# A decoder block with all large products by tokens, and every turn of a result through 32x32 DVE transposes and DRAM

## The chip, the cores and the metric

The kernel runs on one NeuronCore of a Trainium2 chip. The metric is the device time of one execution in microseconds (us). Engines are named as the profile names them: PE (TensorE, the matmuls), PEld (its weight loads), DVE (VectorE), ACT (ScalarE), POOL (GpSimd) and SP (SyncE, which issues transfers here).

## What is computed

One layer on 256 tokens of width 2048, all in float32: a half-step SwiGLU FFN (width 5632), a mixing block, a cross-attention into 256 memory tokens, a second half-step FFN, and a last RMSNorm. Cut to what matters:

```
h = h + 0.5 * swiglu(rms_norm(h, ffn1_norm), w_gate, w_up, w_down)        # (silu(x@w_gate) * (x@w_up)) @ w_down
n = rms_norm(h, mix_norm)
rq, rk, rv, rg, sq, sk, sv = split(n @ w_in)          # 8 heads of retention, 16 + 2 of sliding-window attention
ret = silu(rg) * group_norm(retention(rope(rq), rope(rk), rv))
swa = sliding_window_attention(rope(sq), rope(sk), sv, sinks)
h = h + concat(ret, swa) @ w_out
h = h + memory_cross_attention(rms_norm(h, xa_norm), rms_norm(mem, mem_norm), xa_wq, xa_wkv, xa_wo)   # 4 heads of 512
h = h + 0.5 * swiglu(rms_norm(h, ffn2_norm), ffn2_w_gate, ffn2_w_up, ffn2_w_down)
out = rms_norm(h, final_norm)
```

## The kernel before

**Precision.** Each float32 operand is cut into a high part, rounded to the matmul's format, and a low part, the rest (`halves`: ACT copies the high part, DVE subtracts). A product is three matmuls: high by high, high by low, low by high.

**The stream.** All weights pass once, in pieces of 128x1024 (0.5 MB). SP loads them two at a time into `wf` (three buffers, lines 149 to 161), ACT and DVE cut them into `wh` and `wl` (four buffers, `split`, line 163), and PE uses one piece per *step*. `run_stream` (188) goes through the steps of all *units* in one list; a unit is a set of output columns, summed over its blocks of 512 inputs in a PSUM tile `acc` (two of them). At each step it first runs what is due, then emits the split of the piece three steps ahead (`LOOKAHEAD`), then the step's matmuls. After a unit's last step `done` is called. `later(n, f)` puts f n steps further in the program. Within the first 16 steps two units alternate, and everything is pinned in order there; beyond that a scheduler sets each engine's order.

**Two kinds of step.** *By tokens* (`by_tokens`, 224): the activation's 128 tokens are PE's stationary operand, 512 weight columns move past, and the result has tokens on the partitions: 2 x 2 x 3 = 12 matmuls of 512 columns (lines 408 to 410). *By weights* (`by_weights`, 235): a 128x128 weight tile is stationary, and the activation's high and low parts of 256 tokens move past together: 8 matmuls of 512 columns (243), then 8 of 256 for the low weights (251). The result has features on the partitions, as the next product wants its inputs; the two column halves are summed afterwards (`total`, 399; `add_to_h`, 413). By weights go both down projections of FFN 1, retention's rq and rk, `w_out`, and the keys, queries and output of the cross-attention. The residual `h` lies with features on the partitions (`hT`).

**The turn that exists already.** FFN's gated block comes by tokens and is wanted by features. `up_done` (448) lets DVE transpose its 32x32 squares into `box`, 16 moves on SP's queue (`move`, 459, two to five steps later) shift the squares between partitions, and `made` (464, seven steps later) splits the result. After the cross-attention, `turn_h` (886) turns `h` back with 32 PE transposes.

**Norms.** A norm's scale is applied late. `stat` squares each block on ACT and sums on DVE; after the last one `finish` (line 371) sums over the partitions with four matmuls on PE and takes the power on Pool. `attend` (821) is one head of the cross-attention; `ret_scores` (686) the retention scores of one head.

Of the kernel before, what the change touches and what calls it, by code (L numbers as in the profile page):

```python
# [17 lines left out]
P = 128  # L18
# [13 lines left out]
WARM = 12  # L32
FIRST = 16
SWA_EVERY = 5
# [3 lines left out]
def decoder_block(ctx: ExitStack, tc: tile.TileContext, a: dict, out: bass.AP):  # L38
# [5 lines left out]
    small = ctx.enter_context(tc.tile_pool(name="small", bufs=8))  # L44
    ps_acc = ctx.enter_context(tc.tile_pool(name="ps_acc", bufs=2, space=bass.MemoryType.PSUM))
# [36 lines left out]

    nc.scalar.dma_start(gains, a["gains"])
# [8 lines left out]

# [36 lines left out]
    class Unit:  # L129
# [4 lines left out]
        def __init__(self, w, index, n, lhs, done, blocks, turned=False, per_half=False, pair=False):  # L134
            self.w, self.n, self.lhs, self.done = w[2 * index : 2 * index + 2] if pair else w[index], n, lhs, done
            self.blocks, self.turned, self.per_half, self.pair = list(blocks), turned, per_half, pair
            units.append(self)
# [10 lines left out]

    def load(w, piece, count):
        wf = wpool.tile([P, 2, 1024], F32, tag="wf", name=nm("wf"), bufs=3)  # L150
        nc.sync.dma_start(wf[:, :count, :], w[piece : piece + count].rearrange("c p n -> p c n"))
        return [wf[:, i, :] for i in range(count)]

    def load_pair(w, piece, cuts=(0, 1024)):

        wf = wpool.tile([P, 2, 1024], F32, tag="wf", name=nm("wf"), bufs=3)
        src = w[:, piece].rearrange("f p n -> p f n")
        for lo, hi in zip(cuts, cuts[1:]):
            nc.sync.dma_start(wf[:, :, lo:hi], src[:, :, lo:hi])
        v = wf.rearrange("p f (k n) -> p k f n", n=S)  # L160
        return [v[:, 2 * i : 2 * i + 2] for i in range(2)]

    def split(wf, n, parts):
        wh, wl = (wpool.tile([P, 1024], F32R, tag=x, name=nm(x)) for x in ("wh", "wl"))
        if len(wf.shape) == 4:
            dst = [x.rearrange("p (k f n) -> p k f n", k=2, f=2) for x in (wh, wl)]
            for i in range(parts):
                ks = slice(i * 2 // parts, (i + 1) * 2 // parts)
                halves(dst[0][:, ks], dst[1][:, ks], wf[:, ks])
        else:  # L170
# [5 lines left out]
    def pin():  # L176

        prev = {}
        for ins in nc.cur_bb.bb.instructions:
            if ins.engine in prev:  # L180
# [7 lines left out]
    def run_stream():  # L188
        steps = [x for u in units for x in u.steps()]
        steps[:FIRST] = [x for y in zip(steps[: FIRST // 2], steps[FIRST // 2 : FIRST]) for x in y]  # L190
        loaded = []
        for i in range(0, FIRST, 4):
            cuts = (0, 512, 1024) if i == 0 else (0, 1024)
            for lo, hi in zip(cuts, cuts[1:]):
                load_x(i // 4, lo // S, hi // S)
                if i == 0:
                    if lo == 0:
                        wf = wpool.tile([P, 2, 1024], F32, tag="wf", name=nm("wf"), bufs=3)
                        src = steps[0][0].w[:, steps[0][3]].rearrange("f p n -> p f n")
                    nc.sync.dma_start(wf[:, :, lo:hi], src[:, :, lo:hi])  # L200
            if i == 0:
                v = wf.rearrange("p f (k n) -> p k f n", n=S)
                both = [[v[:, 2 * j : 2 * j + 2] for j in range(2)]]
            else:
                both = [load_pair(steps[i][0].w, steps[i][3])]
            both.append(load_pair(steps[i + 1][0].w, steps[i + 1][3]))
# [4 lines left out]
        def prepare(upto):  # L211
            while nxt[0] < min(upto, len(steps)):
# [8 lines left out]
                ready[at] = split(loaded[at], steps[at][0].n, 2 if at == 0 else 1)  # L221
# [10 lines left out]

        wide_first = [True]

        def by_weights(acc, x, wh, wl, first, last):

            wide = first or (wide_first[0] and not last)
            wide_first[0] = not wide

            def main_pass(closing):  # L240
                for k in range(4):
                    for f in range(2):
                        nc.tensor.matmul(  # L243
                            acc[:, f, :], wh[:, k, f * P : (f + 1) * P], x[:, k, :, :],
                            start=first and k == 0, stop=closing and k == 3,
                        )

            def low_pass():
                for k in range(4):
                    for f in range(2):  # L250
                        nc.tensor.matmul(  # L251
                            acc[:, f, :S], wl[:, k, f * P : (f + 1) * P], x[:, k, 0, :], start=False, stop=False
                        )
            if wide:
                main_pass(False)
                low_pass()
            else:
                low_pass()
                main_pass(last)

        held = []
        for at, (u, b, ks, _, first, last) in enumerate(steps):
# [16 lines left out]
            if u.turned:  # L279
                by_weights(u.acc[0], x, wh, wl, first, last)  # L280
# [16 lines left out]
        run_until(lambda: not tasks)  # L297

# [30 lines left out]
    class Norm:  # L329
# [12 lines left out]
        def block(self, b, src):  # L342

            x = blk()
            k = 0
# [3 lines left out]
            self.blocks[b] = x  # L349
# [44 lines left out]
        def scale_turned(self, x):  # L394
# [4 lines left out]
    def total(acc):  # L399

        x = t2k().rearrange("p (f s) -> p f s", f=2)
        copy(x, acc[:, :, S:])
        nc.vector.tensor_tensor(x, acc[:, :, :S], x, ALU.add)  # L403
# [9 lines left out]
    def add_to_h(j, acc, factor):  # L413

        v = hT[j // 2][:, 2 * (j % 2) : 2 * (j % 2) + 2, :]
        x = t2k().rearrange("p (f s) -> p f s", f=2)
        copy(x, acc[:, :, S:], scale=factor)
        nc.vector.tensor_tensor(v, v, x, ALU.add)  # L418
        nc.vector.scalar_tensor_tensor(v, acc[:, :, :S], factor, v, ALU.mult, ALU.add)  # L419

    def to_h(w, lhs, factor, blocks, norm=None, then=None):

        def done(acc, j):
            add_to_h(j, acc, factor)
            if norm is not None and j % 2 == 1:
                norm.block(j // 2, [hT[j // 2]])
                norm.stat([hT[j // 2]])
            if then is not None:
                then(j)
        for j in range(8):  # L430
            Unit(w, j, 256, lhs, lambda acc, j=j: done(acc, j), blocks, turned=True)

    def ffn(norm, w_gate, w_up, down):
# [12 lines left out]
        def up_done(b):  # L446
            def done(acc):
                s = gated.pop(b)
                box = blk(F32).rearrange("p k c s -> p (k c s)").rearrange("p (w b n) -> p w b n", w=2, b=4)
                squares = box[:, 0].rearrange("p b (q t j) -> p q b t j", q=4, t=2)  # L450
                for t in range(2):
                    nc.vector.scalar_tensor_tensor(s[t], acc[:, t, :], norm.scale(t), s[t], ALU.mult, ALU.mult)  # L452
                    nc.vector.transpose(squares[:, :, :, t, :], s[t].rearrange("p (q b j) -> p q b j", q=4, b=4))  # L453
                for i in range(4):
                    later(2 + i, lambda i=i: move(box, i))
                later(7, lambda: made(b, box))
            return done

        def move(box, i):

            for j in range(4):
                nc.sync.dma_start(box[32 * j : 32 * j + 32, 1, i, :], box[32 * i : 32 * i + 32, 0, j, :])  # L462

        def made(b, box):
            x = blk()
            for t in range(2):
                src = box[:, 1].rearrange("p a (q t j) -> p q t a j", q=4, t=2)[:, :, t]
                hi, lo = (
                    x[:, :, c, t * P : (t + 1) * P].rearrange("p q (a j) -> p q a j", a=4) for c in range(2)
                )  # L470
                halves(hi, lo, src)
            acts[b] = x

        for g, fbs in enumerate((range(0, 6), range(6, 11))):
            for b in fbs:
                Unit(w_gate, b, 512, norm.blocks, gate_done(b), range(4), pair=True)
                Unit(w_up, b, 512, norm.blocks, up_done(b), range(4), pair=True)
            down(g, acts, fbs)
# [557 lines left out]
```

## Time and profile before

| | |
|---|---|
| median of 3 runs (lowest, highest) | 2222.48 us (2220.45, 2222.61) |
| the profiled execution, its span | 2222.29 us, 2220.5 us |
| mean granted TensorE clock | 0.997 |
| matmuls on lines 408, 409, 410 | 2112 each |
| matmuls on lines 243 and 251 | 1984 each |
| moved by DMA, mean rate | 427.04 MB, 192 GB/s |

A row of a group gives line, engine, operation, operands, shape and count, then busy us and mean ns of one, then the idle time of the engine just before, and what ended it. A row of a timeline gives start, length, what, and in brackets the idle time before it. ACTq, SPq and POOLq are the sequencers that issue transfers. In rows of DMA issues the last number is the median time in us from issue to landing.

### The profile page before, as it was taken

What the parts mean: (1) busy time and instruction counts of PE and PEld (TensorE: products, weight loads), DVE (VectorE), ACT (ScalarE), POOL (GpSimd) and SP (SyncE); (2) the same over time, 40 slices, a digit from 0 to 9 for tenths busy, and PEclk for the clock granted to TensorE, in tenths of its full rate; (3) what the DMA queues carried; (4) which work ended last, traced back from release to release, by engine and by line L of the source; (5) the groups of instructions that cost most, each with busy time, mean ns of one, the idle gap of its engine ahead of it and who ended that gap; (6) DMA issues with size and microseconds to landing.
All of it is one profiled execution on the core that took longest, in us unless ns stands there. A gap on an engine that the chain in (4) does not pass through costs nothing.

```text
span 2220.5 us, 27264 instructions
## 1 busy us (share of the span) xinstructions
PE 2199.1 (99%) x10898; PEld 1865.5 (84%) x10898; DVE 1290.8 (58%) x1540; ACT 1035.7 (47%) x1281; POOL 10.3 (0%) x17
## 2 busy tenths in 40 slices
PE   8999999999999999999999999999999999999998
PEld 7788888888888888888888889888888888888886
DVE  5555555455456678886765656664555554555554
ACT  5444434444445565555544554454444433444443
POOL 0000000000000000000000000000000000000000
PEclk9999999999999999999999999999999999999999
DMA  6556555565565554445555544454665565466563
GB/s 241 199 196 224 205 190 181 191 213 185 202 222 197 182 178 163 153 170 190 209 185 191 193 171 152 154 190 163 226 206 186 214 211 195 161 234 208 200 230 133
DMA packets 126527, 427.04 MB, mean 192 GB/s; under 512 B 12608, under 2 KB 23872, under 8 KB 126272
## 3 DMA queue, kind: packets, MB, share of 16 engines
q1 hardware_dynamic: 126256, 425.26, 55.2%
q8 instruction: 85, 1.39, 0.2%
q14 instruction: 42, 0.34, 0.0%
q10 hardware_dynamic: 144, 0.05, 0.0%
HBM read 411.62 MB, written 2.10 MB: 186 GB/s over the span
## 4 chain that ended last, share of the span: by engine, by line
PE 96%; SPq 1%; DMA 1%; DVE 1%; issue 1%; ACT 0%; ACTq 0%; POOLq 0%; POOL 0%
PE acc L410 21%; PE acc L409 21%; PE acc L408 21%; PE acc L243 20%; PE acc L251 10%; SPq L462 1%; DMA wf<-in_ffn_w_up 1%; PE tmp L408 0%; PE tmp L410 0%; PE tmp L409 0%; PE tmp L568 0%; DVE wl L73 0%; PE tmp L594 0%; ACT wh L68 0%; PE tmp L371 0%
## 5 line engine op out<-in xcount | busy, mean ns | idle before, releaser
L73 DVE TENSOR_TENSOR wl<-wf,wh 128x1024 fp32r<-128x1024 f32 (+1 forms) x773 | 936.8, 1221 | 721.0 <-ACT wh L68 715.0
L68 ACT ACTIVATE wh<-wf 128x1024 fp32r<-128x1024 f32 (+1 forms) x773 | 813.2, 1059 | 913.0 <-PE acc L410 609.7
L408 PE MATMUL acc<-wh,blk 128*128 128x512 f32 (+1 forms) x2112 | 821.0, 389 | 4.8 <-ACT wh L68 3.1
L409 PE MATMUL acc<-wl,blk 128*128 128x512 f32 (+1 forms) x2112 | 819.6, 388 | 2.2 <-DVE wl L73 2.2
L410 PE MATMUL acc<-wh,blk 128*128 128x512 f32 (+1 forms) x2112 | 819.4, 388 | 0.1
L243 PE MATMUL acc<-blk,wh 128*128 128x512 f32 x1984 | 480.8, 392 | 0.6 <-ACT wh L68 0.6
L408 PEld LDWEIGHTS acc<-wh,blk 128*128 128x128 f32 x2112 | 396.9, 188 | 86.1 <-ACT wh L68 3.9
L409 PEld LDWEIGHTS acc<-wl,blk 128*128 128x128 f32 x2112 | 397.1, 188 | 84.0 <-DVE wl L73 3.2
L410 PEld LDWEIGHTS acc<-wh,blk 128*128 128x128 f32 x2112 | 397.0, 188 | 81.9 <-DVE blk L327 0.5
L243 PEld LDWEIGHTS acc<-blk,wh 128*128 128x128 f32 x1984 | 364.3, 189 | 70.6 <-ACT wh L68 1.0
L251 PEld LDWEIGHTS acc<-blk,wl 128*128 128x128 f32 x1984 | 257.5, 192 | 15.1 <-ACT blk L68 4.9
L251 PE MATMUL acc<-blk,wl 128*128 128x256 f32 x1984 | 263.5, 284 | 3.8 <-ACT blk L68 3.8
L68 ACT ACTIVATE t2k<-acc 128x512 f32<-128x512 f32 x56 | 33.5, 598 | 126.0 <-PE acc L243 126.0
L418 DVE TENSOR_TENSOR h<-h,t2k 128x512 f32<-128x512 f32 x32 | 22.2, 693 | 53.7 <-ACT t2k L68 53.7
L73 DVE TENSOR_TENSOR blk<-blk,blk 128x512 fp32r<-128x512 f32 x44 | 28.5, 689 | 39.7 <-ACT blk L68 39.7
L68 ACT ACTIVATE blk<-blk 128x512 fp32r<-128x512 f32 x44 | 25.4, 625 | 52.2 <-DMA blk<-blk 52.2
L68 ACT ACTIVATE blk<-tmp 128x512 fp32r<-128x512 f32 (+3 forms) x57 | 26.0, 470 | 26.9 <-DVE blk L73 15.9
L452 DVE SCALAR_TENSOR_TENSOR t2k<-acc,n,t2k 128x512 f32<-128x512 f32 x44 | 31.1, 746 | 8.5 <-PE acc L410 8.5
L403 DVE TENSOR_TENSOR t2k<-acc,t2k 128x512 f32<-128x512 f32 x24 | 16.6, 690 | 32.9 <-ACT t2k L68 32.9
L443 ACT ACTIVATE t2k<-acc,n 128x512 f32<-128x512 f32 x44 | 27.6, 680 | 3.6 <-PE acc L410 3.3
L68 ACT ACTIVATE blk<-h,gains 128x256 fp32r<-128x256 f32 x64 | 28.2, 499 | 1.6 <-DVE h L419 1.6
L453 DVE STREAM_TRANSPOSE blk<-t2k 128x512 f32<-128x512 f32 x44 | 28.6, 686 | 0.0
(130 smaller groups left out, 612.1 us busy)
## 6 DMA issues: line engine op xcount, KB each, us to landing
wf<-in_ffn_w_up SPq DMA_DIRECT2D x88, 1024.0 KB, 5.4
wf<-in_ffn_w_gate SPq DMA_DIRECT2D x87, 1024.0 KB, 5.2
wf<-in_ffn_w_down SPq DMA_DIRECT2D x84, 1024.0 KB, 4.9
wf<-in_w_in_rqk SPq DMA_DIRECT2D x16, 1024.0 KB, 4.9
wf<-in_w_in_rvg SPq DMA_DIRECT2D x16, 1024.0 KB, 4.9
wf<-in_w_out SPq DMA_DIRECT2D x16, 1024.0 KB, 4.9
wf<-in_xa_wk SPq DMA_DIRECT2D x16, 1024.0 KB, 4.9
wf<-in_xa_wv SPq DMA_DIRECT2D x16, 1024.0 KB, 4.9
```

The source lines that it names most:

```text
L68: return nc.scalar.activation(dst, src, AF.Copy, **kw)
L73: nc.vector.tensor_tensor(lo, src, hi, ALU.subtract)
L243: nc.tensor.matmul(acc[:, f, :], wh[:, k, f * P : (f + 1) * P], x[:, k, :, :], start=first and k == 0, stop=closing and k == 3,)
L251: nc.tensor.matmul(acc[:, f, :S], wl[:, k, f * P : (f + 1) * P], x[:, k, 0, :], start=False, stop=False)
L408: nc.tensor.matmul(o, ah, bh, start=start, stop=False)
L409: nc.tensor.matmul(o, ah, bl, start=False, stop=False)
L410: nc.tensor.matmul(o, al, bh, start=False, stop=stop)
L418: nc.vector.tensor_tensor(v, v, x, ALU.add)
L443: nc.scalar.activation(gated[b][t], acc[:, t, :], AF.Silu, scale=norm.scale(t))
L452: nc.vector.scalar_tensor_tensor(s[t], acc[:, t, :], norm.scale(t), s[t], ALU.mult, ALU.mult)
L453: nc.vector.transpose(squares[:, :, :, t, :], s[t].rearrange("p (q b j) -> p q b j", q=4, b=4))
L462: nc.sync.dma_start(box[32 * j : 32 * j + 32, 1, i, :], box[32 * i : 32 * i + 32, 0, j, :])
```

## The change

Everything that went by weights goes by tokens, so it comes out with tokens on the partitions; a new `cross` turns it. For each half of 128 tokens DVE transposes the 32x32 squares of a 128x512 tile, Pool's queue writes the tile to DRAM (256 KB), and four reads from there (64 KB each, runs of 512 bytes) bring it back with rows of squares exchanged. What uses the result stands `TURN` = 4 steps later. `cross` serves the gated blocks (in place of `move`), `to_h`, rq and rk, keys, queries, and `turn_h`. `together` interleaves two units that follow on a turned result: all blocks of both but the last, then the last block of each. The first weight piece and the first `x` are loaded in smaller parts, the first 128 KB of `x` from ACT's queue, and SP's instructions are pinned to program order at the end.

```
-        def __init__(self, w, index, n, lhs, done, blocks, turned=False, per_half=False, pair=False):
+        def __init__(self, w, index, n, lhs, done, blocks, per_half=False, pair=False):
...
+                nx, ny = (sum(z[1] == s[-1][1] for z in s) for s in (x, y))
+                out += x[:-nx] + y[:-ny] + x[-nx:] + y[-ny:]
...
+                for j, lo, hi in ((0, 0, S), (0, S, 2 * S), (1, 0, 2 * S), (0, 2 * S, 1024), (1, 2 * S, 1024)):
+                    if j == 0 and lo > 0:
+                        load_x(0, lo // S, hi // S)
+                    nc.sync.dma_start(dst[j][:, :, lo:hi], src[j][:, :, lo:hi])
...
-            if u.turned:
-                by_weights(u.acc[0], x, wh, wl, first, last)
...
+        pin([mybir.EngineType.SP])
...
+    def cross(src, then, delay=TURN):
+        out = []
+        for v in src:
+            sq, dst = t2k(), t2k()
+            nc.vector.transpose(sq.rearrange("p (g q j) -> p q g j", g=4, q=4), v)
+            box = dram.tile([P, 512], F32, tag="box", name=nm("box"))
+            nc.gpsimd.dma_start(box, sq)
+            far = box.rearrange("(i r) (g n) -> g r i n", i=4, g=4)
+            for g in range(4):
+                nc.gpsimd.dma_start(dst[32 * g : 32 * g + 32, :].rearrange("p (i n) -> p i n", i=4), far[g])
+            out.append(dst.rearrange("p (i q j) -> p q i j", i=4, q=4))
+        later(delay, lambda: then(out))
+
+    def halves_of(out, x):
+        for t in range(2):
+            hi, lo = (x[:, :, c, t * P : (t + 1) * P].rearrange("p q (a j) -> p q a j", a=4) for c in range(2))
+            halves(hi, lo, out[t])
         return x
...
+            cross([squares_of(x) for x in s], add)
+        for b in range(4):
+            Unit(w, b, 512, lhs, lambda acc, b=b: done(acc, b), blocks, pair=True)
...
-                for i in range(4):
-                    later(2 + i, lambda i=i: move(box, i))
-                later(7, lambda: made(b, box))
+                def made(out):
+                    acts[b] = halves_of(out, blk())
+                cross([squares_of(x) for x in s], made)
...
+            s = [scaled(acc, t, 512, norm) for t in range(2)]
+            def made(out):
+                dst[i] = halves_of(out, blk())
                 if then is not None:
                     later(1, then)
-            later(1, finish)
+            cross([squares_of(x) for x in s], made)
...
-        tp = [tmp_ps() for _ in range(2)]
-        for t in range(2):
-            for k in range(4):
-                nc.tensor.transpose(tp[t][:, k * P : (k + 1) * P], hT[b][:, k, t * P : (t + 1) * P], ident)
-            copy(h[t][:, b * 512 : (b + 1) * 512], tp[t])
+        def made(out):
+            for t in range(2):
+                copy(squares_of(h[t][:, b * 512 : (b + 1) * 512]), out[t])
+        cross([hT[b][:, :, t * P : (t + 1) * P].rearrange("p q (a j) -> p q a j", a=4) for t in range(2)], made)
```

How the change moves instructions, at three places. First SP at the first down projection of FFN 1, before; `wf` are the loads of weights, `blk` the turn of the last gated block.

```order
L159 DMA wf_1917<-in_ffn_w_up 128x2x1024
L151 DMA wf_1951<-in_ffn_w_down 128x2x1024
L151 DMA wf_1985<-in_ffn_w_down 128x2x1024
L151 DMA wf_2029<-in_ffn_w_down 128x2x1024
L151 DMA wf_2079<-in_ffn_w_down 128x2x1024
L462 DMA blk_2003<-blk_2003 32x256 x16
L151 DMA wf_2129<-in_ffn_w_down 128x2x1024
L151 DMA wf_2181<-in_ffn_w_down 128x2x1024
```

SP there after the change:

```order
L178 DMA wf_1914<-in_ffn_w_up 128x2x1024
L178 DMA wf_1948<-in_ffn_w_down 128x2x1024
L178 DMA wf_1982<-in_ffn_w_down 128x2x1024
L178 DMA wf_2037<-in_ffn_w_down 128x2x1024
L178 DMA wf_2071<-in_ffn_w_down 128x2x1024
L178 DMA wf_2110<-in_ffn_w_down 128x2x1024
L178 DMA wf_2144<-in_ffn_w_down 128x2x1024
```

The 16 moves are gone from SP; the turn of a gated block now stands on Pool's queue as one write and four reads per half, in series.

Second, DVE between the end of a query's unit and its scores in the first `attend`, before: `acc` is the unit's sum, `wl` are splits of weights, line 403 is `total`, and line 833 is the maximum over the scores.

```order
L403 TENSOR_TENSOR t2k_10464<-acc_10379,t2k_10464 128x512
L397 TENSOR_TENSOR t2k_10464<-t2k_10464,rows_9058 128x512
L73 TENSOR_TENSOR wl_10468<-wf_10442,wh_10467 128x1024
L73 TENSOR_TENSOR wl_10494<-wf_10491,wh_10493 128x1024
L73 TENSOR_TENSOR blk_10397<-t2k_10464,blk_10397 128x2x256
L73 TENSOR_TENSOR wl_10549<-wf_10491,wh_10548 128x1024
L833 TENSOR_REDUCE xm_10538<-tmp_10513 128x2
```

DVE there after the change; line 417 is the transpose of one half in `cross`.

```order
L417 STREAM_TRANSPOSE t2k_9937<-t2k_9933 128x4x4x32
L75 TENSOR_TENSOR wl_9956<-wf_9915,wh_9955 128x1024
L75 TENSOR_TENSOR wl_9975<-wf_9972,wh_9974 128x1024
L417 STREAM_TRANSPOSE t2k_9946<-t2k_9935 128x4x4x32
L75 TENSOR_TENSOR wl_9991<-wf_9972,wh_9990 128x1024
L75 TENSOR_TENSOR wl_10009<-wf_10006,wh_10008 128x1024
L75 TENSOR_TENSOR blk_10024<-t2k_9938,blk_10024 128x4x128
L75 TENSOR_TENSOR wl_10030<-wf_10006,wh_10029 128x1024
L75 TENSOR_TENSOR wl_10083<-wf_10080,wh_10082 128x1024
L75 TENSOR_TENSOR blk_10024<-t2k_9947,blk_10024 128x4x128
L843 TENSOR_REDUCE xm_10070<-tmp_10045 128x2
```

Two transposes, two splits of weights apart, are new. Six splits of weights lie between the first of them and the maximum's row, where three lay between the sum and that row; the low part of each half stands four splits behind its transpose.

Third, PE at the same `attend`, before: `acc` rows are the next unit's steps, `tmp` rows of lines 408 to 410 are the scores.

```order
L243 MATMUL acc_10379<-blk_10278,wh_10375 128x512 x8
L243 MATMUL acc_10471<-blk_10144,wh_10402 128x512 x8
L251 MATMUL acc_10471<-blk_10144,wl_10403 128x256 x8
L251 MATMUL acc_10471<-blk_10187,wl_10423 128x256 x8
L243 MATMUL acc_10471<-blk_10187,wh_10422 128x512 x8
L408 MATMUL tmp_10513<-blk_9061,blk_10397 128x256
L409 MATMUL tmp_10513<-blk_9061,blk_10397 128x256
```

PE there after the change, from the last matmuls ahead of the scores:

```order
L434 MATMUL acc_9959<-wh_9974,blk_9739 128x512
L435 MATMUL acc_9959<-wl_9975,blk_9739 128x512
L436 MATMUL acc_9959<-wh_9974,blk_9739 128x512
L434 MATMUL tmp_10045<-blk_8764,blk_10024 128x256
L435 MATMUL tmp_10045<-blk_8764,blk_10024 128x256
L436 MATMUL tmp_10045<-blk_8764,blk_10024 128x256
```

Two steps of the next unit stood ahead of the scores; now it is five steps of 12 matmuls, 60 in all, and four more between the scores of the two halves of the tokens.

238 lines of the change are left out of this document (109 added, 129 removed).

## The prediction

> **What bounds the kernel now.** I read the page first: which engine fills the span, and what the chain that ended last is made of.
>
> ```profile
> span 2220.5 us, 27264 instructions
> PE 2199.1 (99%) x10898; PEld 1865.5 (84%) x10898; DVE 1290.8 (58%) x1540; ACT 1035.7 (47%) x1281; POOL 10.3 (0%) x17
> PE 96%; SPq 1%; DMA 1%; DVE 1%; issue 1%; ACT 0%; ACTq 0%; POOLq 0%; POOL 0%
> ```
>
> TensorE is busy 99% of the span and is 96% of the chain. So only two things can move the time: how long PE needs for the same products, and how long it stands still. Everything on DVE (58%), ACT (47%), the queues and Pool counts only where PE waits for it. The profiled execution took 2222.3 us, 1.8 more than its span; the median of the three runs is 2222.48, so the sum is made against 2222.3. About 0.2% (4.4 us) is what a measurement here can tell from no change.
>
> The second view is the groups: products by weights run from two lines.
>
> ```profile
> L243 PE MATMUL acc<-blk,wh 128*128 128x512 f32 x1984 | 480.8, 392 | 0.6 <-ACT wh L68 0.6
> L251 PE MATMUL acc<-blk,wl 128*128 128x256 f32 x1984 | 263.5, 284 | 3.8 <-ACT blk L68 3.8
> ```
>
> Matmuls overlap in the records, so 392 and 284 ns aren't prices. The price is the distance between starts. The chain, in order of time, gives it for the stage by weights (start, length, what):
>
> ```profile
> 301.41 1.91 PE acc L251 x16
> 303.32 3.65 PE acc L243 x16
> 306.98 1.91 PE acc L251 x16
> ```
>
> 16 narrow and 16 wide matmuls, two steps of the program, take 306.98 - 301.41 = 5.57 us: 2.78 us a step. The timeline of PE in a stage by tokens:
>
> ```profile
> 1599.81 0.39 PE L410 MATMUL acc<-wh,blk 128*128 128x512 f32 x1
> 1600.03 0.39 PE L408 MATMUL acc<-wh,blk 128*128 128x512 f32 x1
> ...
> 1616.81 0.39 PE L410 MATMUL acc<-wh,blk 128*128 128x512 f32 x1
> ```
>
> 75 starts lie between the first and the last of these rows: 17.00 / 75 = 0.2267 us. A step by tokens has 12 of them: 2.72 us.
>
> **The change part by part.**
>
> *All large products by tokens.* L243 has 1984 matmuls, 8 a step: 248 steps. Each becomes 12 matmuls of 512 columns in place of 8 of 512 and 8 of 256. The columns streamed are the same (6144); four matmuls fewer start. 248 x (2.783 - 2.720) = **-15.5 us**, all on the path, since PE is the path. [...]
>
> *The first units of both down projections of FFN 1.* Here PE stands still today, because the last gated block isn't turned yet:
>
> ```profile
> 291.51 1.11 PE L251 MATMUL acc<-blk,wl 128*128 128x256 f32 x8
> 295.16 2.07 PE L251 MATMUL acc<-blk,wl 128*128 128x256 f32 x8 [2.53 <-ACT blk L68]
> 651.37 0.73 PE L243 MATMUL acc<-blk,wh 128*128 128x512 f32 x2 [0.57 <-ACT wh L68]
> 653.36 2.08 PE L251 MATMUL acc<-blk,wl 128*128 128x256 f32 x8 [1.26 <-ACT blk L68]
> 281.98 10.31 SPq L462 DMA_DIRECT2D blk<-blk  x15
> 293.95 1.15 ACT L68 ACTIVATE blk<-blk 128x512 fp32r<-128x512 f32 x2 [2.99 <-DMA blk<-blk]
> ```
>
> Idle 2.53 and 0.57 + 1.26, 4.4 us. A unit has one step per block now and two after, so the last block is wanted after 10 and 8 steps instead of 5 and 4, 27 and 22 us. The round trip below needs about 16. **-4.4 us.** What is late next is nothing on PE: the weights no longer queue behind 16 moves on SP.
>
> *The moves leave SP.* Once they cost PE time away from a down projection, and the same rows measure how late ACT may be:
>
> ```profile
> 64.82 10.12 SPq L462 DMA_DIRECT2D blk<-blk  x16
> 71.04 1.06 ACT L68 ACTIVATE wh<-wf 128x1024 fp32r<-128x1024 f32 x1 [1.66 <-PE acc L410]
> 76.55 1.16 ACT L68 ACTIVATE blk<-blk 128x512 fp32r<-128x512 f32 x2 [4.45 <-DMA blk<-blk]
> 80.36 2.01 ACT L68 ACTIVATE wh<-wf 128x1024 fp32r<-128x1024 f32 x2 [2.66 <-DMA wf<-in_ffn_w_up]
> 82.74 0.50 PE L409 MATMUL acc<-wl,blk 128*128 128x512 f32 x1 [0.63 <-DVE wl L73]
> ```
>
> The split due at 71.04 + 2.72 = 73.76 came at 80.36, 6.6 us late, and PE lost 0.6: a split may be 6 us late for nothing. That is the cover of every ACT or DVE instruction that will wait for a round trip. **-0.6 us.** An issue on SP is 10.12/16 = 0.63 us.
>
> *turn_h.* Its 32 PE transposes go to DVE, eight at a time between two products:
>
> ```profile
> 1530.18 1.03 PE L892 MATMUL tmp<-ident,h 128*128 128x128 f32 x8
> 1530.97 0.48 PE L408 MATMUL acc<-wh,blk 128*128 128x512 f32 x1
> ```
>
> 4 x 0.79 = **-3.2 us**.
>
> *Smaller first loads.* PE's and ACT's first rows:
>
> ```profile
> 5.99 1.15 ACT L68 ACTIVATE wh<-wf 128x512 fp32r<-128x512 f32 x2 [3.54 <-DMA wf<-in_ffn_w_gate]
> 7.60 0.50 PE L408 MATMUL acc<-wh,blk 128*128 128x512 f32 x1 [1.73 <-ACT blk L68]
> 12.02 1.06 ACT L68 ACTIVATE wh<-wf 128x1024 fp32r<-128x1024 f32 x1 [3.27 <-DMA wf<-in_ffn_w_up]
> 13.13 0.50 PE L408 MATMUL acc<-wh,blk 128*128 128x512 f32 x1 [2.18 <-ACT wh L68]
> 14.39 0.50 PE L409 MATMUL acc<-wl,blk 128*128 128x512 f32 x1 [0.76 <-DVE wl L73]
> 18.38 0.40 PE L410 MATMUL acc<-wh,blk 128*128 128x512 f32 x1
> ```
>
> and the windows of 10 us (start:end, length, PE busy):
>
> ```profile
> 30.00:40.00 10.00, 10.00 (x46) 8.28 (x45) 7.59 (x11) 7.81 (x12) 0.00 (x0) 1.00 0.69 256
> ```
>
> PE starts after 768 KB, then waits 2.18 + 0.76 us for the next piece (2.5 MB issued by then), and after it runs slow: ten starts from 14.39 to 18.38 take 3.99 us, not 2.27. Afterwards the first piece is 384 KB and the second comes after 1.3 MB. If all goes (1.3 earlier by halved bytes, 2.9, 1.7) it is -5.9; if the loads that follow limit PE, 0. I take **-4**, near the full end, because in the windows that follow PE is busy throughout at 256 GB/s.
>
> *New: the round trips.* 54 of them (22 gated blocks, 16 output blocks of to_h, 4 rotary, 4 keys, 4 queries, 4 turn_h), each for two halves: one DVE transpose, a 256 KB write to DRAM, and four reads of 64 KB that Pool may issue only when the write has landed. The trace has no Pool DMA. The nearest rows:
>
> ```profile
> blk<-blk SPq DMA_DIRECT2D x352, 32.0 KB, 1.8
> out<-t2k SPq DMA_DIRECT2D x8, 256.0 KB, 2.5
> t2k<-in_mem SPq DMA_DIRECT2D x8, 256.0 KB, 5.7
> L453 DVE STREAM_TRANSPOSE blk<-t2k 128x512 f32<-128x512 f32 x44 | 28.6, 686 | 0.0
> L68 ACT ACTIVATE blk<-h,gains 128x256 fp32r<-128x256 f32 x64 | 28.2, 499 | 1.6 <-DVE h L419 1.6
> L356 ACT ACTIVATE t2k<-h 128x512 f32<-128x512 f32 x32 | 19.5, 621 | 0.0
> L360 DVE TENSOR_TENSOR t2k<-t2k,t2k 128x512 f32<-128x512 f32 x35 | 23.8, 686 | 0.3
> L68 ACT ACTIVATE t2k<-acc,nmix 128x512 f32<-128x512 f32 x8 | 5.2, 682 | 3.7 <-PE acc L410 3.7
> L73 DVE TENSOR_TENSOR wl<-wf,wh 128x1024 fp32r<-128x1024 f32 x771 | 935.5, 1222 | 716.1 <-ACT wh L68 710.0 <-PE acc L410 2.6
> ```
>
> At SP's prices a half takes 2.5 + 3 x 0.63 + 1.8 = 6.2 us and holds Pool for 5.0. Behind the waiting read on Pool stand the second half's write and reads, then the powers of the norms. Gated blocks: their copies stand four splits (10.9 us) after the transposes, with 6 us of cover behind; nothing.
>
> Where PE itself is next, there is less room. First query: ACT copies and DVE turns half one by 0.3 + 0.68 + 0.69 = 1.7 us after the unit; half two stands behind two splits, about 5.7; Pool is free at 6.7, so half two lands at 12.9 and is split (0.6 + 0.7) at 14.2. PE's order has 60 matmuls (13.6 us) before the scores, and the second half's scores come 2.3 later: 15.9. Room 1.7. The three later attends also pass 24 matmuls of 0.12 us: room 3.7. For the sums of the mix norm: landing 13.5, one add, four gained copies (0.50), two squares (0.62), one add (0.69), 18.1 against 19.7 of PE work; for the memory-attention norm 15.5 against 17.9; the two retention scores about 16.9 against 18.5. Rooms 1.6, 2.4, 1.6, 1.6. Lower end: 0 (a dependence added can't be a gain; what it replaced is counted above). Half two lands later by nearly ten times what each Pool DMA costs beyond SP's 0.63. At +0.35 (3.3 later): 1.6 + 1.7 + 0.9 + 2 x 1.7 = 7.6. At the 5.7 us of the row of in_mem for write and reads, 10 later: 8.3 + 3 x 6.3 + 8.4 + 7.6 + 2 x 8.4 = 60. I take **+7**: the out row, the same size and the only write to DRAM, is the nearest one, and its price leaves all rooms open; half as much again per issue is my allowance for another issuer and for weights on the same engines. [...]
>
> DVE and ACT bind nowhere new: 64 more transposes are 44 us on DVE, and the summing of halves that goes (two DVE operations fewer for each 512 columns) gives about as much back. What the trips write and read, 27 MB each way, I hold hidden: the loads wait for PE today, not PE for them.
>
> Sum: 2222.3 - 15.5 - 4.4 - 0.6 - 3.2 - 4 + 7 = **2201.6 us**, say 2201.
>
> **The rivals.**
>
> *Pool is late: slower.* Each Pool DMA is dearer by 0.63 us or more. From there (half two 5.7 later: 4 + 3 x 2 + 4 + 3.3 + 2 x 4 = 25, with the first FFN's crowding) the eight places eat the 27.7 us of gains. At +0.9: 6.8 + 3 x 4.8 + 7 + 6 + 2 x 7 = 48, 2243 us. [...] Against: six of eight places need over 1.6 us of lateness to cost anything. [...] Chance 0.16.
>
> *Pool is as cheap as SP.* No new wait: 2194; with the full start gain 2192. For it: the rooms computed. Chance 0.2.
>
> *The matmul order pays nothing.* [...] Against: both distances are measured in this kernel. 0.05.
>
> *In between*, 2218 to 2227: several rooms overdrawn by some 4 us. 0.07.
>
> **How the numbers follow.** The forecast's case (2195 to 2213) has 0.52. Range 2188 to 2226: from no new wait with all of the start and some of the small gaps around attention, to the in-between case; it leaves out most of the slower rival. Faster 0.77 (0.52 + 0.2 + 0.05), same 0.07, slower 0.16.
>
> **What would show it.** Right: 3104 matmuls on each of the three by-token lines at 0.227 us; no idle PE at the first units of w_down; first product near 6 us; PE idle before the scores of attends, the norm sums and retention scores of under 3 us each. Wrong: Pool reads issued over 1 us apart, landings over 20 us after the unit's end, or PE waits for ACT blk or DVE in more than eight places.

## The result, and the profile after

The changed kernel takes **2288.03 us** (median of 4 runs, 2286.74 to 2290.45) against 2221.47 us for the kernel before in the same comparison (4 runs, 2220.39 to 2222.61): the ratio is 1.030, with a 95% interval of 1.028 to 1.032. The forecast was 2201 us with a range to 2226. The time moved the other way, and by three times as much as was forecast.

The page of the changed kernel first, its span and its first line of busy times:

```profile
span 2286.7 us, 25822 instructions
PE 2203.9 (96%) x9868; PEld 1821.7 (80%) x9868; DVE 1290.5 (56%) x1532; ACT 1023.8 (45%) x1257; POOL 309.0 (14%) x557
```

Before, PE was busy 99% of 2220.5 us, which leaves 21 us; now 96% of 2286.7, which leaves 83. DVE and ACT do no more work than before (1290.5 against 1290.8 us, 1023.8 against 1035.7). No engine became the bound: PE stands still. Which waits, the view of waits on PE tells (who waits, for whom; total us, times, longest):

```profile
PE acc L434 <- ACT wh L70: 22.1, 5, 13.6
PE tmp L377 <- DVE t2k L366: 15.4, 3, 8.9
PE acc L434 <- ACT t2k L470: 11.4, 1, 11.4
PE acc L435 <- DVE wl L75: 8.9, 9, 1.7
PE tmp L705 <- DVE blk L696: 6.4, 1, 6.4
PE tmp L434 <- ACT blk L70: 3.5, 3, 3.1
```

In rows two, five and six PE itself uses what a round trip brings (norm sums, retention scores, scores of the queries). The largest row is something else: PE waits for `wh`, the high part of an ordinary piece of weights, five times and up to 13.6 us. In the two long ones (13.6 and 4.7 us) the weights had been loaded but not *cut*. In the third row it waits for ACT to empty a sum, which ACT comes to late. The groups on the page say why (busy us and mean ns, then the idle time of the engine just before them and what ended it):

```profile
L434 PE MATMUL acc<-wh,blk 128*128 128x512 f32 (+1 forms) x3104 | 1215.4, 392 | 34.4 <-ACT wh L70 22.1
L422 POOL DMA_DIRECT2D t2k<-box x432 | 235.8, 553 | 397.6 <-DMA box<-t2k 222.3
L419 POOL DMA_DIRECT2D box<-t2k x108 | 61.2, 567 | 1343.7 <-DVE t2k L417 1341.3
L70 ACT ACTIVATE blk<-t2k 128x512 fp32r<-128x512 f32 (+2 forms) x74 | 46.1, 623 | 194.7 <-DMA t2k<-box 192.8
L445 DVE TENSOR_TENSOR h<-h,t2k 128x512 f32<-128x512 f32 x32 | 22.1, 691 | 70.8 <-DMA t2k<-box 70.8
```

ACT stood 192.8 us in front of copies whose trip hadn't landed, DVE 70.8 us in front of adds to `h`. Both engines also cut the weights, in one line with those copies and adds. On Pool an issue costs 553 and 567 ns. The landings are in the rows of DMA issues:

```profile
box<-t2k POOLq DMA_DIRECT2D x108, 256.0 KB, 3.4
t2k<-box POOLq DMA_DIRECT2D x432, 64.0 KB, 3.5
```

The write of 256 KB takes 3.4 us at the median where 2.5 were assumed, a read of 64 KB 3.5 where 1.8 were assumed. From the first write of a trip to the last landing of its second half, the 54 trips of this trace take 12.6 us at the shortest, 16.2 at the median and 22.4 at the longest (start of the write row on Pool to the last landing of the reads of the same tile).

**Where the time went.** For the table I counted the columns that PE's matmuls into `acc` had streamed, and read when each kernel had reached a given share of them; that puts the same work side by side although the kernels wait at different places. The third column is e5, below, in which nothing waits for a trip and SP isn't pinned. Both are differences against the kernel before, negative is ahead; the last column is what the changed kernel loses against e5 in the stretch.

| share, and what lies before it | changed, us | e5, us | lost in this stretch |
|---|---|---|---|
| 0.30, FFN 1, first unit of the second down projection | -13.0 | -13.1 | |
| 0.34, rest of that down projection | -7.7 | -15.2 | 7.4 |
| 0.36, mix norm | -4.0 | -16.2 | 4.7 |
| 0.46, attention and retention | 8.1 | -16.2 | 12.1 |
| 0.50, `w_out` and memory norm | 39.2 | -12.1 | 27.0 |
| 0.66, keys, values, queries, columns of `xa_wo` | 42.6 | -17.1 | 8.4 |
| 0.72, start of FFN 2: last adds of `xa_wo`, norm, turn of `h` | 59.2 | -20.8 | 20.3 |
| 1.00, FFN 2 | 65.6 | -20.8 | 6.4 |

Up to 0.30 the kernel runs ahead as forecast. All of the loss comes after it, most of it at places at which the forecast had put nothing.

One of the small places in full, the second unit of that down projection (640 to 690 us). The timeline of the changed kernel, rows of SP, Pool, DVE, ACT and PE:

```profile
649.97 0.46 SPq L514 DMA_DIRECT2D blk<-in_dmat  x1
...
660.54 0.56 POOL L419 DMA_DIRECT2D box<-t2k  x1
667.80 2.18 POOL L422 DMA_DIRECT2D t2k<-box  x4 [6.70 <-DMA box<-t2k]
...
664.78 0.69 DVE L445 TENSOR_TENSOR h<-h,t2k 128x512 f32<-128x512 f32 x1 [4.39 <-DMA t2k<-box]
665.39 2.35 DVE L75 TENSOR_TENSOR wl<-wf,wh 128x1024 fp32r<-128x1024 f32 x2
674.57 0.69 DVE L445 TENSOR_TENSOR h<-h,t2k 128x512 f32<-128x512 f32 x1 [6.83 <-DMA t2k<-box]
...
675.30 1.70 ACT L70 ACTIVATE blk<-h,gains 128x256 fp32r<-128x256 f32 x4 [10.72 <-DVE h L445]
677.95 3.88 ACT L70 ACTIVATE wh<-wf 128x1024 fp32r<-128x1024 f32 x4
...
679.04 0.79 PE L434 MATMUL acc<-wh,blk 128*128 128x512 f32 x1 [4.68 <-ACT wh L70]
```

Read from the end: PE stands 4.68 us for a piece of weights. ACT cuts it only now, because the gained copies of `h` stand ahead of it, and those waited 10.72 us for DVE's add. DVE stood 6.83 us in front of that add, for half two of the trip: its write was issued at 660.54, and the reads behind it could go only at 667.80. The first half's write landed after 3.56 us, with the load of `dmat` (1 MB, landed at 657.08) and from 655.96 a load of weights under way; the second half's after 6.98 us, with two loads of weights under way.

### The profile page after: what moved, and what is told of

The parts are those of the page before. It is cut to its first block, busy times and chain, and to the rows that moved or that the text cites. A ratio compares the mean times of both kernels' runs of the same rounds, so it can differ in the third digit from the quotient of the medians.

```text
span 2286.7 us, 25822 instructions
## 1 busy us (share of the span) xinstructions
PE 2203.9 (96%) x9868; PEld 1821.7 (80%) x9868; DVE 1290.5 (56%) x1532; ACT 1023.8 (45%) x1257; POOL 309.0 (14%) x557
## 4 chain that ended last, share of the span: by engine, by line
PE 41%; DMA 5%; issue 3%; POOL 2%; ACT 1%; DVE 1%; ACTq 0%; POOLq 0%; DVEq 0%
PE acc L435 13%; PE acc L436 13%; PE acc L434 13%; DMA t2k<-box 3%; DMA box<-t2k 2%; POOL t2k L422 2%; ACT wh L70 1%; DVE wl L75 0%; ACT blk L70 0%; PE tmp L436 0%; PE tmp L377 0%; PE tmp L434 0%; PE tmp L435 0%; DVE t2k L366 0%; ACT t2k L70 0%
## 5 line engine op out<-in xcount | busy, mean ns | idle before, releaser
L434 PE MATMUL acc<-wh,blk 128*128 128x512 f32 (+1 forms) x3104 | 1215.4, 392 | 34.4 <-ACT wh L70 22.1
L435 PE MATMUL acc<-wl,blk 128*128 128x512 f32 (+1 forms) x3104 | 1213.8, 391 | 8.9 <-DVE wl L75 8.9
L436 PE MATMUL acc<-wh,blk 128*128 128x512 f32 (+1 forms) x3104 | 1211.9, 390 | 0.0
L434 PEld LDWEIGHTS acc<-wh,blk 128*128 128x128 f32 x3104 | 587.3, 189 | 158.0 <-ACT wh L70 24.7
L435 PEld LDWEIGHTS acc<-wl,blk 128*128 128x128 f32 x3104 | 587.3, 189 | 133.1 <-DVE wl L75 13.6
L436 PEld LDWEIGHTS acc<-wh,blk 128*128 128x128 f32 x3104 | 587.4, 189 | 121.4 <-DVE blk L75 0.4
L422 POOL DMA_DIRECT2D t2k<-box x432 | 235.8, 553 | 397.6 <-DMA box<-t2k 222.3
L419 POOL DMA_DIRECT2D box<-t2k x108 | 61.2, 567 | 1343.7 <-DVE t2k L417 1341.3
L70 ACT ACTIVATE blk<-t2k 128x512 fp32r<-128x512 f32 (+2 forms) x74 | 46.1, 623 | 194.7 <-DMA t2k<-box 192.8
L75 DVE TENSOR_TENSOR blk<-t2k,blk 128x512 fp32r<-128x512 f32 (+1 forms) x66 | 44.7, 678 | 131.7 <-ACT blk L70 131.5
L445 DVE TENSOR_TENSOR h<-h,t2k 128x512 f32<-128x512 f32 x32 | 22.1, 691 | 70.8 <-DMA t2k<-box 70.8
L417 DVE STREAM_TRANSPOSE t2k<-t2k 128x512 f32<-128x512 f32 x76 | 53.6, 705 | 13.4 <-ACT t2k L70 13.4
L470 ACT ACTIVATE t2k<-acc,n 128x512 f32<-128x512 f32 x44 | 27.7, 682 | 16.8 <-PE acc L436 16.7
L329 DVE SCALAR_TENSOR_TENSOR blk<-h,gains,blk 128x256 fp32r<-128x256 f32 x64 | 27.0, 480 | 2.4 <-ACT blk L70 2.4
```

Of the source, the lines that this page charges most:

```text
L70: return nc.scalar.activation(dst, src, AF.Copy, **kw)
L75: nc.vector.tensor_tensor(lo, src, hi, ALU.subtract)
L329: nc.vector.scalar_tensor_tensor(x[:, k, 1, :], v[:, k, :], g, x[:, k, 0, :], ALU.mult, ALU.subtract)
L417: nc.vector.transpose(sq.rearrange("p (g q j) -> p q g j", g=4, q=4), v)
L419: nc.gpsimd.dma_start(box, sq)
L422: nc.gpsimd.dma_start(dst[32 * g : 32 * g + 32, :].rearrange("p (i n) -> p i n", i=4), far[g])
```

## The experiments

Times are medians; the ratio is to the kernel before in the same comparison, with its 95% interval. Theory A: ACT and DVE stand in line behind a trip, the cutting of weights stands behind that, and PE runs dry. Theory B: the 54 MB of the trips make the weights late. Theory C: SP, now in program order, holds weights behind other loads at `w_out`.

**e1, nothing waits for a trip.** The edit:

```
-            out.append(dst.rearrange("p (i q j) -> p q i j", i=4, q=4))
+            out.append(sq.rearrange("p (g q j) -> p q g j", g=4, q=4))
```

Expected:

> Every round trip still runs (108 writes, 432 reads), but what uses the result takes DVE's own transpose instead, so nothing waits for a trip; the exchange of rows of squares is left out of the computation. Theory A (ACT and DVE stand in line behind a trip, the splits of weights stand behind that, and PE runs dry): the some 75 us of PE idle at the turns go, 2200 to 2212 us. Theory B (54 MB more on the DMA engines makes the weights late): the time stays within 15 us of the changed kernel, 2273 to 2290. Theory C (SP in program order holds weights behind other loads around w_out): 2235 to 2260, since only what isn't at w_out goes.

Measured: 2211.69 us, ratio 0.996 (0.995 to 0.998). The trips all run (Pool is busy 306.9 us), and the loss is gone, as theory A has it: 2288.0 - 2211.7 = 76 us hang on waits for the trips, and theory B is out. At `w_out` it still falls back, from 18.7 us ahead of before at 0.46 to 4.6 at 0.50.

**e5, the same without the pin on SP** (`pin([mybir.EngineType.SP])` left out as well).

> As e1 (nothing waits for a trip, which leaves the exchange of rows out of the computation), with SP's order left to the scheduler. e1 still lost some 14 us at w_out. Theory C (there, SP in program order stands at the loads of mem, which wait for a buffer, and the weights queue behind them): 2196 to 2202 us. Rival (the adds and norm sums themselves crowd DVE and ACT at w_out): 2208 to 2214.

Measured: 2200.55 us, ratio 0.991 (0.989 to 0.992). What the change gains by itself, with neither the waits nor the pin, is 19.5 us, and all that it loses is 2288.03 - 2200.55 = 87.5. The pin alone has a price of 11 us even where no trip is waited for. The busy times of e5:

```profile
PE 2179.9 (99%) x9868; PEld 1810.2 (82%) x9868; DVE 1293.4 (59%) x1532; ACT 1029.4 (47%) x1257; POOL 307.1 (14%) x557
```

The changed kernel has the same 9868 matmuls, and PE is busy with them for 2203.9 us. So of the 87 us between the two spans (2286.7 and 2200.1) some 63 are PE standing still (83 us idle against 20), and 24 are PE working more slowly; the granted clock, 0.982 on the mean against 0.996, is taken up further down.

**e2, both halves written before either is read.**

```
             nc.gpsimd.dma_start(box, sq)
+            trips.append((dst, box))
+        for dst, box in trips:
             far = box.rearrange("(i r) (g n) -> g r i n", i=4, g=4)
```

> Both halves are written before either is read. From the first write to the last landing the changed kernel took 16.2 us at the median; now the second write no longer stands behind four reads, so about 11.5. Theory A: each of some eight stalls gets 4 to 5 us shorter, 2245 to 2260 us. Theory B: the same bytes at nearly the same time, 2280 to 2292. Theory C: 2280 to 2292.

Measured: 2242.28 us, ratio 1.011 (1.009 to 1.013): 46 us less for another order of ten issues, and 3 us under the band of theory A. The trips took 13.5 us at the median instead of 16.2, not the 11.5 I had expected: eight reads in a row take 5.0 us each to land. In its rows of DMA issues the write is faster, the read slower, and the sum better:

```profile
box<-t2k POOLq DMA_DIRECT2D x108, 256.0 KB, 2.9
t2k<-box POOLq DMA_DIRECT2D x432, 64.0 KB, 5.0
```

**e6, half the weights.** Only the first half of every later piece is loaded: 

```
-        nc.sync.dma_start(wf, w[:, piece].rearrange("f p n -> p f n"))
+        nc.sync.dma_start(wf[:, :, :512], w[:, piece].rearrange("f p n -> p f n")[:, :, :512])
...
-        return [v[:, 2 * i : 2 * i + 2] for i in range(2)]
+        return [v[:, :2] for i in range(2)]
```

> Of every later piece of weights only the first half is loaded and used twice (half of the weights is left out of the computation); the order of all instructions and all waits stay. If the trips are long because weights are under way on the same DMA engines, the median from the first write to the last landing falls from 16.2 us towards the 12.5 of the shortest ones, and the time to 2240 to 2265 us. If a trip is long by itself (issues in series on Pool and the landings of small transfers): 15 to 16 us, and 2275 to 2290.

Measured: 2236.71 us, ratio 1.008 (1.006 to 1.009), a little below the band; the trips took 13.3 us at the median. Its rows of DMA issues, with every issue on SP and Pool in the changed kernel's order:

```profile
box<-t2k POOLq DMA_DIRECT2D x108, 256.0 KB, 2.6
t2k<-box POOLq DMA_DIRECT2D x432, 64.0 KB, 2.5
```

So what else was under way lengthened the trips here (16.2 us at the median with all of the weights, 13.3 with half). In the changed kernel's own trace the writes during which no load of SP was under way (3 to 6, by where one lets a load begin) landed after 2.31 to 2.38 us, and such reads (13 to 24) after 2.14 to 2.28; the others, on Pool's queue and not on that of the loads all the same, took up to 7.8 and 7.7. `w_out` still lost 24 of its 31 us in e6, so most of its loss is not a matter of bytes.

**e3, SP unpinned.**

> SP's order is the scheduler's again, all else as changed. Theory A: no cause of the loss, 2275 to 2295 us. Theory B: the same. Theory C: the 31 us lost around w_out mostly come back, 2253 to 2268.

Measured: 2261.99 us, ratio 1.018 (1.017 to 1.020). At `w_out` it lost 10 us (3.1 ahead at 0.46, 7.1 behind at 0.50) where the changed kernel lost 31. With e1 and e5 this gives all four corners: waiting for the trips costs 76 us with the pin and 2262.0 - 2200.6 = 61 without it; the pin costs 26 us with the waits and 11 without them (the kernel before took 2220 to 2222 us in each of these comparisons). e3 also lost nothing at the place shown above. The timeline of e3, the same rows:

```profile
658.09 0.56 POOL L418 DMA_DIRECT2D box<-t2k  x1
661.88 2.17 POOL L421 DMA_DIRECT2D t2k<-box  x4 [3.23 <-DMA box<-t2k]
...
661.25 0.69 DVE L444 TENSOR_TENSOR h<-h,t2k 128x512 f32<-128x512 f32 x1 [2.05 <-DMA t2k<-box]
667.57 0.69 DVE L444 TENSOR_TENSOR h<-h,t2k 128x512 f32<-128x512 f32 x1 [0.20 <-issue]
...
665.10 1.05 SPq L513 DMA_DIRECT2D blk<-in_dmat  x1
```

`dmat`'s 1 MB is asked for at the end of the trip instead of just ahead of it (665.10 against 649.97). The trip takes 14.0 us instead of 20.2, the second add waits for nothing, and PE doesn't stop. That `dmat` made the trip long is not shown: in the changed kernel it had landed before half two was written. DVE also cuts three pieces between the two adds here, where it cut two. But e6, with the changed kernel's order on DVE up to there, had a trip of 11.7 us at this place, and PE didn't stop either: the length is enough by itself.

**e13, other buffers for the loads of `mem`, the pin kept.** Why would SP's order matter at `w_out`? The timeline of the changed kernel there, SP, DVE, ACT and PE:

```profile
1066.54 7.59 SPq L782 DMA_DIRECT2D t2k<-in_mem  x2
1074.18 0.94 SPq L178 DMA_DIRECT2D wf<-in_w_out  x2
...
1073.90 2.32 DVE L75 TENSOR_TENSOR wl<-wf,wh 128x1024 fp32r<-128x1024 f32 x2
1082.94 0.69 DVE L445 TENSOR_TENSOR h<-h,t2k 128x512 f32<-128x512 f32 x1 [6.72 <-DMA t2k<-box]
1093.93 0.69 DVE L445 TENSOR_TENSOR h<-h,t2k 128x512 f32<-128x512 f32 x1 [8.11 <-DMA t2k<-box]
1097.34 4.63 DVE L75 TENSOR_TENSOR wl<-wf,wh 128x1024 fp32r<-128x1024 f32 x4
...
1094.72 1.15 ACT L362 ACTIVATE t2k<-h 128x512 f32<-128x512 f32 x2 [9.83 <-DVE h L445]
1095.77 3.89 ACT L70 ACTIVATE wh<-wf 128x1024 fp32r<-128x1024 f32 x4
...
1096.87 0.80 PE L434 MATMUL acc<-wh,blk 128*128 128x512 f32 x1 [13.62 <-ACT wh L70]
```

Two loads of `mem` stand 7.59 us on SP, and the weights of `w_out` come only behind them, at 1074.18. Those loads go into `t2k`, of which there are ten; a trip holds four. From 1030 to 1130 us the loads of `mem` wait on SP 25.6 us for writes and reads of trips to land, and 18.5 until DVE has summed a norm's squares, which lie in `t2k` too. DVE cuts no piece from 1076.2 to 1097.3: it waits 6.72 us for half one and 8.11 for half two, with no cut between. ACT stands 9.83 us for the second add, to square its sum, and cuts only behind that. The order that the scheduler made had put the cuts into clumps of four behind both adds. e13 puts those loads into a `blk` buffer:

```
-        m = [t2k().rearrange("p (k s) -> p k s", k=2) for _ in range(2)]
+        room = blk(F32).rearrange("p k c s -> p (k c s)")
+        m = [room[:, 512 * i : 512 * i + 512].rearrange("p (k s) -> p k s", k=2) for i in range(2)]
```

> SP stays pinned in the same order; the loads of mem go into buffers of the blk kind instead of t2k, which the trips use four at a time. If what holds SP at w_out is that a load of mem waits for a t2k buffer that a trip keeps: the 27 us at w_out fall to 5 to 12, 2265 to 2276 us. If the pinned order by itself is late there: 2283 to 2292.

Measured: 2275.5 us, ratio 1.023 (1.020 to 1.027), with one of four runs at 2262.3. At `w_out` 10.8 us are lost instead of 31 (6.4 behind at 0.46, 17.2 at 0.50). The timeline of e13, DVE at the same adds:

```profile
1080.08 0.69 DVE L445 TENSOR_TENSOR h<-h,t2k 128x512 f32<-128x512 f32 x1 [1.79 <-DMA t2k<-box]
1080.69 1.22 DVE L75 TENSOR_TENSOR wl<-wf,wh 128x1024 fp32r<-128x1024 f32 x1
...
1084.02 1.22 DVE L75 TENSOR_TENSOR wl<-wf,wh 128x1024 fp32r<-128x1024 f32 x1
1092.31 0.69 DVE L445 TENSOR_TENSOR h<-h,t2k 128x512 f32<-128x512 f32 x1 [7.07 <-DMA t2k<-box]
```

The second add still waits 7.07 us, but two pieces are cut between the adds. SP's pinned order is the same in both, and the loads of `mem` now wait 0.4 us in all. So it is the shared buffers under a pinned order, not the order by itself. How they cost time is not parted further: from this place on the scheduler also put DVE's and ACT's instructions into another order. Of the 20 us that came back there, 8 were lost again at other trips further on, mostly at the turn of `h` (from 0.66 to 0.72 e13 loses 24.9 us, the changed kernel 16.6); that shift is not explained.

**e4, users held back.** TURN 6, and on ACT and DVE the first use of a trip's result may not be moved ahead of what the program emitted earlier:

```
-TURN = 4
+TURN = 6
...
+            for x in ins[n:]:
+                if x.engine in (mybir.EngineType.Activation, mybir.EngineType.DVE):
+                    tc.add_manual_dep(x, last[x.engine].name, ..., reason="program order")
```

> TURN is 6, and on ACT and DVE what uses a trip's result may not be moved ahead of what the program emitted before it (the scheduler put it two to four splits behind the transposes whatever TURN said; now four or more stand ahead of it). Theory A: the splits run on while the trip is under way; the stalls at the adds of w_out and at 674 us go for the most part, 35 to 55 us less, 2233 to 2253 us. Theory B: 2280 to 2295. Theory C: 2275 to 2290.

Measured: 2240.98 us, ratio 1.010 (1.008 to 1.012), in the band of theory A. The trips are as long as ever (17.1 us at the median), the loss at 674 us is gone, `w_out` loses 12 instead of 31. What it costs: at the mix norm, where PE has nothing else left, it loses 8 (14.5 ahead at 0.34, 6.3 at 0.36).

**e9, TURN 6 alone.**

> TURN is 6 instead of 4 and nothing else. In DVE's order the users of the gated blocks' trips stay where they were (the scheduler, not TURN, had put them two to four splits behind the transposes). If what counts is where a user stands in DVE's and ACT's order: only the places gain at which PE itself uses a trip, 2262 to 2285 us. If TURN alone moves the wait out of the way: as e4, 2235 to 2250.

Measured: 2254.46 us, ratio 1.015 (1.013 to 1.017): between my two bands, and neither reading holds as I had put it. Up to 674 us the order on DVE is row for row the old one; the stall there is gone all the same. TURN also delays the request for `dmat`, to 656.52 us, the trip takes 16.2 instead of 20.2, and a third piece is cut ahead of the second add; which of these did it, this run doesn't tell. From the mix norm to the end of the retention, where TURN moved PE's own places, 15 us came back (14.9 ahead at 0.34 and 13.6 at 0.46, against 7.7 ahead and 8.1 behind); `w_out` still loses 21.

**e8, `w_out` by weights; e10, `h` turned on PE.** Each undoes one place, with the functions of the kernel before.

> w_out alone goes by weights as before, without its four trips; all else as changed. Theory A with C (of the 66 us some 31 are lost between 0.46 and 0.50 of the columns, around w_out): 2255 to 2263 us, with 2 us of the slower step given back. Theory B (traffic): 2284 to 2290.

> The last turn of h goes back to 32 PE transposes, without its four trips. They stand where the changed kernel lost 11.6 us (0.68 to 0.70 of the columns). If these four trips are the cause: about 9 us less with 3.2 given back to PE, 2273 to 2282. If the queue of ACT's work there is late without them: 2288 to 2293.

Measured: e8 2254.01 us, ratio 1.016 (1.013 to 1.018), 34 us less; `w_out` loses nothing (3.0 behind before and after it). e10 2273.13 us, ratio 1.023 (1.021 to 1.024), 14.9 us less. e8 is 1 us under its band, e10 at the lower edge of its first one. e8's 34 us are about what the changed kernel falls back at `w_out` (31). Of what e10 gains, by the columns 8 us come back from 0.66 to 0.72 and 6 in FFN 2.

**e7, everything mended but the trips themselves.** e2's writes, e4's holding back with TURN 4, e3's free SP, e10's turn.

> Writes first, users of a trip not moved ahead of earlier work (TURN stays 4), SP unpinned, and h turned on PE as before the change. If the losses add up (writes first 46, SP's order some 15 of what is then left, h's turn 6): 2213 to 2225 us. If they are one and the same stall, counted several times: 2230 to 2245.

Measured: 2229.75 us, ratio 1.005 (1.003 to 1.007): 4.8 us over the band for losses that add up and 0.3 under the one for a stall counted several times. The single mendings e2, e3, e4 and e10 gave 46, 26, 47 and 15 us, all together give 58: in large part they take back the same loss. By the columns e7 still loses 10 us at the norm sum behind `xa_wo` (a wait of 7.8), 6 at the retention scores and 6 at the norm behind `w_out`, places at which PE itself waits for what a trip brings.

**e11 and e12, trips only where they are hidden.** By weights again, as before the change: `w_out` and `xa_wo`, in e12 retention's rq and rk too; `h` turned on PE; writes first; SP free. Trips stay for the gated blocks, both down projections of FFN 1, keys and queries, in e11 for rq and rk as well.

> Trips only where six or more splits of work lie behind them: gated blocks, both down projections of FFN 1, rotary parts, keys and queries; w_out and xa_wo go by weights again, h turns on PE, writes first, SP unpinned. From where e1 and e2 stand at 0.46 of the columns (10 us ahead of before) with 4 us of cadence given back and 2 to 4 lost at the rotary parts: 2205 to 2214 us. If the losses move to the remaining trips as in e7: 2216 to 2224.

> As e11, and retention's rq and rk by weights too. Without the waits at the retention scores: 2 to 5 us under e11 by theory A, 2203 to 2210; equal to e11 if those waits were nothing.

Measured: e11 2213.04 us, ratio 0.996 (0.995 to 0.998); **e12 2208.22 us, ratio 0.993 (0.992 to 0.995)**, faster than both kernels. Both lie in the band of their first reading. From the page of e12:

```profile
span 2206.1 us, 26337 instructions
PE 2186.4 (99%) x10284; PEld 1831.5 (83%) x10284; DVE 1285.6 (58%) x1524; ACT 1036.7 (47%) x1281; POOL 220.3 (10%) x397
L70 ACT ACTIVATE blk<-t2k 128x512 fp32r<-128x512 f32 (+1 forms) x66 | 40.9, 620 | 140.6 <-DMA t2k<-box 138.7
```

PE is at 99% again, while ACT still stands 138.7 us in front of trips. Those waits cost next to nothing: PE is idle for 20 us of this span, as it is in e5, where nothing waits for a trip.

## Why the prediction was wrong

**The cadence (-15.5): right.** From 0.14 to 0.18 of the columns, in the first down projection, the changed kernel gains 2.0 us. That is 0.04 of 776 steps (3104 matmuls on each line, four a step), 31 steps: 0.064 us a step against 0.063 forecast.

**The first units of the down projections (-4.4): right, too small.** From 0.12 to 0.14 the lead grows by 4.9 us and from 0.28 to 0.30 by 4.3, about 9 with some 1 us of cadence in it. The term counted idle time. Behind its stops PE here also ran at a lower granted clock: in the windows of the kernel before (the clock is the last column but two) it is 0.79 where PE stood still, and 1.00 from 285 to 292 and from 300 to 310 us:

```profile
292.00:300.00 8.00, 5.47 (x25) 4.71 (x24) 2.74 (x4) 2.58 (x4) 0.00 (x0) 0.79 0.84 309
```

In the changed kernel's windows it is 0.66 behind the stops at the start, and 0.50 behind the stop of 13.62 us:

```profile
13.00:18.00 5.00, 4.37 (x12) 3.48 (x13) 4.83 (x8) 4.83 (x8) 0.00 (x0) 0.66 0.67 220
...
1097.00:1101.00 4.00, 3.05 (x7) 2.06 (x8) 4.00 (x5) 4.00 (x7) 0.00 (x0) 0.50 0.05 12
```

The long stops so cost more than their waits: 45 us of PE's busy time fall in stretches at 0.50 (one lies from 676.4 to 683.2 us, with 3.70 us busy), in e5 10. The 35 us more at half the clock are, as an estimate, 18 of the 24 us by which PE is busy longer here.

**Smaller first loads (-4): right in sign, less than half in size.** 1.5 us by 0.12 of the columns, and 0.1 to 4.6 in the other kernels with the same start. PE starts 2.4 us earlier and then waits for `x` and the next pieces, as its timeline shows:

```profile
5.23 0.77 PE L434 MATMUL acc<-wh,blk 128*128 128x512 f32 x1
...
8.54 0.50 PE L434 MATMUL acc<-wh,blk 128*128 128x512 f32 x1 [0.70 <-ACT blk L70]
...
12.37 0.51 PE L434 MATMUL acc<-wh,blk 128*128 128x512 f32 x1 [1.91 <-ACT wh L70]
13.63 0.50 PE L435 MATMUL acc<-wl,blk 128*128 128x512 f32 x1 [0.75 <-DVE wl L75]
```

The slow ten starts, of which I had counted 1.7 us as a gain, stay: the granted clock from 13 to 18 us is 0.69 in the kernel before and 0.66 here.

**The turn of `h` (-3.2): right for PE.** In e5 the lead grows by 3.7 us from 0.66 to 0.72. **The moves off SP (-0.6)** can't be told apart at this size. Together the gains were forecast at 27.7 us; e5, which has them all, shows 19.5.

**The round trips (+7): wrong.** Waiting for them costs 76 us (e1), and with the 11 of the pin the loss is 87.5. This is the step that failed, in two parts. The length: half two landing "12.9" after the unit's end, with 3.3 us allowed beyond, was worked out from the rows of `out`, written at the very end when no weights are loaded any more, and of moves of 32 KB. Measured, 16.2 us from the first write in place of 11.2, up to 22.4. The 0.35 us more an issue, from which the 3.3 came, no run shows: the issues on Pool, where I had put the risk, took 0.55 us, less than the 0.63 that I had read off SP's moves. By my own list of eight places 5 us more would still have cost only 20 (five rooms of 1.6 to 2.4 overdrawn by 2.6 to 3.4, three of 3.7 by 1.3).

The second part is the cover: "a split may be 6 us late for nothing. That is the cover of every ACT or DVE instruction that will wait for a round trip." I measured that cover at one wait, and then gave it to every user and looked only at places where PE itself uses a trip. Two of ACT's or DVE's waits can follow one another with no cut between (6.72 and 8.11 us at `w_out`), a user can stand behind another user (ACT's gained copies behind DVE's add, 10.72 us), and where the scheduler puts a user isn't where TURN says. The adds to `h` at `w_out` (27 us) and the turn of `h` (15 by e10) weren't on my list at all. I had also left SP's pin unpriced; with shared buffers it held back weights. The two parts work together: shorter trips alone took back 46 and 51 us (e2, e6), users standing further back 47 with trips as long as ever (e4).

The rival "Pool is late" had the sign, at 0.16; issues dearer than SP's by 0.63 us or more the trace doesn't show: none on Pool took longer than 0.73 us. Among the signs named for being wrong, "landings over 20 us" (5 of 54 trips, counted from the first write) and more than eight waits are what the trace shows.

## What to carry to other kernels

Price a new wait on the engine that waits, by what stands behind it in that engine's order and when that is due; a bottleneck engine can be starved by its helpers though it never uses the late result (here PE stood up to 13.6 us for a piece of weights). Take a transfer's latency from rows in which as much else is under way as there will be, and look at its spread: here, for the write, 2.3 us with no load of SP under way, 3.4 at the median, 7.8 at worst. In this kernel a round trip through DRAM was nearly free where enough prepared work lay ahead of the bottleneck (e12); at the other places the older form was faster.

## What the runs showed of the hardware

On Pool's queue an issue took 0.55 us, and a transfer of 64 or 256 KB landed after 2.1 to 7.8 us, the late ones with loads of weights under way. The same trips from another queue were not run. Halving the weights' bytes took the read of 64 KB from 3.5 to 2.5 us. Eight reads issued in a row landed later each (5.0 us at the median), and yet the trip was over sooner (13.5 us against 16.2).
